# Pinning every engine of a hybrid-decoder step to an order planned from measured durations

## The chip, the cores and the metric

One core of a Trainium2 chip runs one program. Its engines are named as in the profile: PE (matrix products; PEld loads the stationary operand), DVE (vector), ACT (scalar), POOL (GpSimd) and SP (which here only issues DMAs). Each takes its instructions strictly from its own queue, in the order in which the program holds them. The metric is the device time of one execution in microseconds (us), median of several runs.

## The reference

One inference step of one layer, for a prompt of 512 positions and 8 sample positions with the same weights, width 1024, all fp32:

```
proj = rms_norm(x) @ w_in                  # 3 x (q,k,v of 512), r,k,v of 1024, loras, two gates of 1024
o_a  = three dilated-window attentions (8 heads x 64), merged by softmax of their log-sums
# RWKV-7, 16 heads x 64, token by token:
sa = S @ (-kk_t)
S  = S * w_t + outer(sa, kk_t * a_t) + outer(v_t, k_t)
y_t = S @ r_t
o_b = (group_norm(y) + bonus) * gate
x   = x + (sigmoid(gate_a) * (o_a @ w_proj_a) + sigmoid(gate_b) * (o_b @ w_proj_b)) @ w_out
x   = x + (silu(h @ w_gate) * (h @ w_up)) @ w_down         # h = rms_norm(x), width 2816
y   = rms_norm(x)
```

The sample positions also read a key/value cache of 128 rows for each attention group and a matrix state for each RWKV head. New keys, values, shift and states are outputs.

## The kernel before

**Layout and the wide products.** Activations lie with features on the 128 partitions and the 520 positions (512 + 8) along the free axis, in two halves of 260 columns. Each weight matrix is cut into blocks of 128 output features. An fp32 product is made of three faster ones: a block's weights `raw` (512 KB, loaded by SP) are split by ACT into a rounded copy `whi` and by DVE into the rest `wlo = raw - whi`, the activations are held as two such parts (`hh`, `hl`; later `fh`, `fl`, `h2h`, `h2l`), and PE adds up hh·whi, hl·whi and hh·wlo. A block is thus 8 x 3 products for each half, 48 *wide* products of 128x128 weights by 260 columns, into a PSUM tile `mm`. `raw`, `whi` and `wlo` have two buffers each, so the split of a block runs while PE works on the block before. In order the blocks are: 36 of attention, 3 of loras, 24 of RWKV (k, r, v of each pair of heads, called p0 to p7), 16 of gates (g0 to g15), w_proj_a, w_proj_b, w_out, then the FFN.

**The small products.** Between the blocks stand generators with products of other shapes, and of transposes, which also take PE out of its wide shape: attention scores (`ch<-qk`), transposes (`ax<-ident,..`) and the RWKV work of each pair. For a pair, `pair(p)` makes AR, BK and the tiles GH on DVE and PE; `solve(p)` inverts small triangular matrices by 31 steps of two DVE instructions (`xt = X·LT`, `X = X + xt`), each needing the one before, with DMA round trips before (TD, LT) and after (TE, GH) on SP's queue; `chain(p)` walks over 8 chunks: PE VTr·GH and AR·AR, ACT to GH, PE GH·KB, DVE to AR, then the next chunk. `merge()` joins the three attention groups; its tiles `oo` and `fb` are loaded by POOL and used at once by DVE (`oo`, `oac`). `sample_group` works on the cache (`kt`, `sc`, `so`).

**What sets the order.** The main generator `play(jobs)` and the small generators are woven together while the program is written: `Weave.run` keeps an estimated clock for each engine (`Clocks`), and steps the generator whose inputs are ready. Every engine call goes through `Unit.__getattr__.call` (line 380, `r = f(*a, **k)`), which prices it, moves the clocks and emits it; the profile therefore shows nearly every instruction under L380, and tiles are told apart by name. The order in which the calls are made is the priority of an instruction; the framework's scheduler then fixes each engine's queue from priorities and its own costs. The constants TIMED and PIN are 0, so neither of the two other ways of setting an order is in use.

```
def wsplit(w, raw, k0, k1, cols=128):
    hi, lo, raw = (t[:, k0:k1, :cols] for t in (*w, raw))
    S.copy(out=hi, in_=raw)
    V.tensor_tensor(out=lo, in0=raw, in1=hi.bitcast(FP), op=ALU.subtract)
```

Of the kernel before, what the change touches and what calls it, by code (L numbers as in the profile page):

```python
# [1 line left out]

# [37 lines left out]
MERGE_AT = -1  # L40
SAMPLE_AT = -1
PLAIN = 4
EARLY = 3
FETCH = 2
SOLVERS = 2
# [1 line left out]
GRAIN = 2  # L47
SOLVE = 3
AHEAD = 0
TIMED = 0  # L50
PIN = 0
WARM = 0.65
TURNS = 4
L_SEM = 0.2

# [170 lines left out]
class Clocks:  # L226


    def __init__(self):
        self.t = dict(PE=0.0, DVE=0.0, ACT=0.0, POOL=0.0, SP=0.0)  # L230
        self.gaps = {e: [] for e in self.t}
        self.work = []
        self.tick, self.columns, self.hot = 0, 0.0, False
        self.done, self.used, self.prev = {}, {}, {}

    @staticmethod
    def region(x):
# [9 lines left out]

    @staticmethod
    def last(d, engine, r=None):
        t = 0.0  # L250
        for q, (end, by, late) in d.items():
            if r is None or (q[0] < r[1] and r[0] < q[1] and q[2] < r[3] and r[2] < q[3]):
                t = max(t, end + (late if by != engine else 0.0 if by == "PE" else 0.12))
        return t

    def free(self, name, engine, r=None):

        if name not in self.done and name in self.prev:
            name, r = self.prev[name], None
        return max(self.last(d.get(name, {}), engine, r) for d in (self.done, self.used))  # L260

    def at(self, x, engine="PE"):

# [33 lines left out]
            del self.work[0]  # L297
        return sum(w for _, w in self.work) / 3.4

    def run(self, engine, outs, ins, price, issue=None, late=L_SEM):  # L300
        start = max([self.at(x, engine) for x in ins if x.name in self.done] +
                    [self.free(x.name, engine, self.region(x)) for x in outs])
        start = self.place(engine, start, price if issue is None else issue)
        end = start + price
        for x, d in [(x, self.used) for x in ins] + [(x, self.done) for x in outs]:
            d.setdefault(x.name, {})[self.region(x)] = end, engine, late
        return start


class Pool:  # L310


    def __init__(self, pool, ck):
        self.pool, self.ck, self.hist = pool, ck, {}

    def tile(self, shape, dtype, name=None, tag=None, bufs=1):
        t = self.pool.tile(shape, dtype, name=name, tag=tag or name, bufs=bufs)
        h = self.hist.setdefault(tag or name, [])
        if len(h) >= bufs:
            self.ck.prev[t.name] = h[-bufs]  # L320
        h.append(t.name)
        return t

# [6 lines left out]
class Unit:  # L330


    def __init__(self, name, engine, tc, ck, keep=None):
        self.name, self.engine, self.tc, self.ck, self.keep = name, engine, tc, ck, keep

    def price(self, op, outs, ins):
        n = max(x.free_size() for x in outs + ins)
        if self.name == "ACT":
            return 0.06 + n / 1200
        if self.name == "POOL":  # L340
            return 0.25 + n / 480
        if self.name != "PE":
            return 0.07 + n / 960
        n = outs[0].free_size()
        if op == "transpose":
            return 0.054 + n / 2400
        if ins[0].dtype == FR:
            return max(0.054, n / 2400)
        if ins[0].partition_size() > 64:
            return 0.085 + 4 * max(0, n - 32) / 2400  # L350
        return max(0.054, 0.028 + 2 * n / 2400)

    def __getattr__(self, op):
        f = getattr(self.engine, op)

        def call(*a, **k):
            aps = list(a)
            outs = [k[x] for x in ("out", "accum_out") if x in k] or [aps.pop(0)]
            ins = [x for x in aps + [v for n, v in k.items() if n not in ("out", "accum_out")] if isinstance(x, bass.AP)]
            if op == "dma_start":  # L360
                kb = outs[0].nbytes() / 1e3
                pool = self.name == "POOL"
                t = self.ck.run(self.name, outs, ins, (2.7 if pool else 1.6) + kb / 360, 1.04 if pool else 0.45, 0.8)
            else:
                if op == "matmul":
                    ins = ins[::-1] if ins[0] is k.get("rhs") else ins
                p = self.price(op, outs, ins)
                if self.name == "PE":
                    self.ck.beat(self.ck.t["PE"])
                    w = outs[0].free_size() * (4 if ins[0].dtype == FP else 1) / 2400 * ins[0].partition_size() / 128  # L370
                    if op == "transpose":
                        w = 0.0
                    t = self.ck.run(self.name, outs, ins, p if self.ck.hot else 2 * p)
                    self.ck.beat(t, w)
                    self.ck.work.append((t, w))
                else:
                    t = self.ck.run(self.name, outs, ins, p)
            if TIMED:
                self.tc.cur_priority = int(t * TIMED)
            r = f(*a, **k)  # L380
            return self.keep(r) if self.keep else r
        return call


# [81 lines left out]
def program(tc, I, O):  # L466
    nc = tc.nc
    ck = Clocks()
    V, S, G, SY = (Unit(n, e, tc, ck) for n, e in (("DVE", nc.vector), ("ACT", nc.scalar), ("POOL", nc.gpsimd), ("SP", nc.sync)))

    E = Unit("PE", nc.tensor, tc, ck, tc.keep_in_program_order if PIN else None)
    X = mybir.AxisListType.X
    ctx = ExitStack()
    wv = Weave(ck, tc)
# [2 lines left out]
    def nm(s):  # L477
        uid[0] += 1
        return f"{s}_{uid[0]}"

    def pool(name, stack, **kw):
        return Pool(stack.enter_context(tc.tile_pool(name=name, bufs=1, reuse_waits="tile", **kw)), ck)

    cp = pool("const", ctx)
    wp = pool("w", ctx)
    mmp = Pool(ctx.enter_context(tc.tile_pool(name="mm", bufs=1, space=PSUM)), ck)
    axp = Pool(ctx.enter_context(tc.tile_pool(name="ax", bufs=1, space=PSUM)), ck)
    chp = Pool(ctx.enter_context(tc.tile_pool(name="ch", bufs=1, space=PSUM)), ck)
    drp = Pool(ctx.enter_context(tc.tile_pool(name="dr", bufs=1, space=DRAM)), ck)

    def const(name, shape, src=None, eng=None):
        t = cp.tile(shape, FP, name=name)
# [3 lines left out]
    def bank():  # L496
        return axp.tile([128, 512], FP, name=nm("ax"), tag="ax", bufs=3)
# [28 lines left out]
    class Part:  # L526


        def __init__(self, i):
            self.i = i  # L530
# [173 lines left out]
    def norm0():  # L704
        banks = yield from norm_r(n0, [acc0], slice(0, NT), TB, "n0")
        for a, b, pb in banks:
            S.copy(out=rs0[:, a:b], in_=pb[:, :b - a])
        wv.set("rs0")
        for k in range(KD):
            t = n0.tile([128, NT], FP, name=nm("hn"), tag="sq0", bufs=2)  # L710
            V.scalar_tensor_tensor(out=t[:], in0=xt[:, k], scalar=feat[:, F_MIX, k:k + 1], in1=rs0[:],
                                   op0=ALU.mult, op1=ALU.mult)
            split(hh[:, k], hl[:, k], t[:], (V, G)[k % 2])
            yield (hl[:, k],)
# [278 lines left out]
    rw = {}  # L993
# [78 lines left out]
    def gates2():  # L1072
        raw = lora_load(0, 2)
        for p in range(NP):
# [5 lines left out]
            yield lo, st3, BANK  # L1080
# [51 lines left out]
    def pair(p):  # L1132
# [7 lines left out]
        yield lo, BANK  # L1140
# [4 lines left out]
        yield (BANK,)  # L1145
        za = small([(hi[:, 1], LA), (lo[:, 1], LA)])
        ta = full("ta")
        for c in range(2):
# [341 lines left out]
    def merge():  # L1490
# [3 lines left out]
        for i in range(2):  # L1494
            yield stat, BANK
            ps = bank()
            for b in range(4):
                E.transpose(ps[:8, b * 128:(b + 1) * 128], stat[:, 0, i, b], ident[:])
            S.copy(out=nat[:, i], in_=ps[:8].rearrange("p (l r) -> p r l", r=4))
            ps = bank()  # L1500
# [467 lines left out]
```

## Time and profile before

| | |
|---|---|
| median of 3 runs (lowest, highest) | 1315.46 us (1314.71, 1316.59) |
| the profiled execution's own time | 1316.53 us |
| its span, first to last instruction | 1314.8 us |
| busy: PE, DVE, ACT, POOL | 1264.7, 843.7, 610.6, 175.0 us |
| mean granted clock of PE | 0.983 |

The profiled execution is 1.1 us above the median, and 1.7 us of it lie outside the span. I cut the span into four stretches: I, to 359 us (attention blocks, loras, first pairs); II, 359 to 558 us (18 blocks, pairs mostly overlapping each other); III, 558 to 838 us (24 blocks: the last pairs, gates, w_proj_a, w_proj_b up to the point where little but wide products is left); IV, 838 us to the end (rest, almost wholly FFN). The borders are the starts of the splits (`wlo`) of the 46th, 64th and 88th weight block, counted in order on DVE, so that the same points can be found in the changed program.

### The profile page before, as it was taken

What the parts mean: (1) busy time and instruction counts of PE and PEld (TensorE: products, weight loads), DVE (VectorE), ACT (ScalarE), POOL (GpSimd) and SP (SyncE); (2) the same over time, 40 slices, a digit from 0 to 9 for tenths busy, and PEclk for the clock granted to TensorE, in tenths of its full rate; (3) what the DMA queues carried; (4) which work ended last, traced back from release to release, by engine and by line L of the source; (5) the groups of instructions that cost most, each with busy time, mean ns of one, the idle gap of its engine ahead of it and who ended that gap; (6) DMA issues with size and microseconds to landing.
All of it is one profiled execution on the core that took longest, in us unless ns stands there. A gap on an engine that the chain in (4) does not pass through costs nothing.

```text
span 1314.8 us, 29468 instructions
## 1 busy us (share of the span) xinstructions
PE 1264.7 (96%) x11738; PEld 1197.5 (91%) x11738; DVE 843.7 (64%) x2221; ACT 610.6 (46%) x1554; POOL 175.0 (13%) x261
## 2 busy tenths in 40 slices
PE   7999999999989989999999999999999999999996
PEld 7998999989978878888888888999999999999996
DVE  6956866954869998886986665555843444332333
ACT  5244244366656656675785665334433232222220
POOL 1300100100223332121123122110200000000000
PEclk9999999999989999997999999999999999999998
DMA  6523654634245554543245454552222222223331
GB/s 215 158 94 96 213 178 146 221 112 172 69 131 136 152 147 141 143 156 97 77 139 168 123 175 157 182 192 85 81 97 97 97 89 89 97 93 89 89 101 65
DMA packets 92137, 169.48 MB, mean 129 GB/s; under 512 B 42416, under 2 KB 47568, under 8 KB 92000
## 3 DMA queue, kind: packets, MB, share of 16 engines
q1 hardware_dynamic: 60880, 102.46, 24.6%
q0 software_dynamic: 14512, 46.47, 11.5%
q10 hardware_dynamic: 16608, 18.68, 4.3%
q8 instruction: 92, 1.51, 0.5%
q14 instruction: 45, 0.37, 0.1%
HBM read 133.20 MB, written 27.94 MB: 123 GB/s over the span
## 4 chain that ended last, share of the span: by engine, by line
PE 64%; DVE 15%; issue 9%; DMA 6%; ACT 4%; POOL 1%; SPq 1%; ACTq 0%; DVEq 0%; POOLq 0%
PE mm L380 51%; PE ax L380 8%; PE ch L380 5%; DVE wlo L380 2%; DVE X L380 1%; DVE xt L380 1%; DMA fb<-FD 1%; DMA sw<-raw 1%; ACT KB L380 1%; DVE k L380 1%; DMA raw<-w_in 1%; SPq L380 1%; DVE raw L380 1%; DVE qk L380 1%; DVE GH L380 1%
## 5 line engine op out<-in xcount | busy, mean ns | idle before, releaser
L380 PE MATMUL mm<-hh,whi 128*128 128x260 f32 x1136 | 340.2, 299 | 0.8 <-ACT gt L380 0.8
L380 PE MATMUL mm<-hh,wlo 128*128 128x260 f32 x1136 | 325.4, 286 | 4.3 <-DVE wlo L380 4.3
L380 PE MATMUL mm<-hl,whi 128*128 128x260 f32 x1136 | 325.7, 287 | 0.0
L380 ACT CAST whi<-raw 128x1024 fp32r<-128x1024 f32 (+1 forms) x165 | 170.1, 1032 | 324.4 <-PE mm L380 290.6
L380 DVE TENSOR_TENSOR wlo<-raw,whi 128x1024 fp32r<-128x1024 f32 (+1 forms) x165 | 197.9, 1199 | 140.2 <-ACT whi L380 137.0
L380 PEld LDWEIGHTS mm<-hh,whi 128*128 128x128 f32 x1136 | 215.7, 190 | 13.3 <-issue 6.0
L380 PEld LDWEIGHTS mm<-hh,wlo 128*128 128x128 f32 x1136 | 215.4, 190 | 6.5 <-DVE wlo L380 5.8
L380 PEld LDWEIGHTS mm<-hl,whi 128*128 128x128 f32 x1136 | 215.5, 190 | 1.4 <-issue 0.2
L380 PE MATMUL mm<-h2l,whi 128*128 128x260 f32 x608 | 171.5, 282 | 0.0
L380 PE MATMUL mm<-h2h,wlo 128*128 128x260 f32 x608 | 171.4, 282 | 0.0
L380 PE MATMUL mm<-h2h,whi 128*128 128x260 f32 x608 | 171.4, 282 | 0.0
L380 PEld LDWEIGHTS mm<-h2h,wlo 128*128 128x128 f32 x608 | 114.5, 188 | 0.0
L380 PEld LDWEIGHTS mm<-h2l,whi 128*128 128x128 f32 x608 | 114.4, 188 | 0.0
L380 PEld LDWEIGHTS mm<-h2h,whi 128*128 128x128 f32 x608 | 114.4, 188 | 0.0
L380 PE MATMUL mm<-fh,wlo 128*128 128x260 f32 x388 | 109.6, 282 | 0.0
L380 PE MATMUL mm<-fh,whi 128*128 128x260 f32 x388 | 109.5, 282 | 0.0
L380 PE MATMUL mm<-fl,whi 128*128 128x260 f32 x388 | 109.5, 282 | 0.0
L380 PEld LDWEIGHTS mm<-fh,whi 128*128 128x128 f32 x388 | 73.1, 188 | 0.0
L380 PEld LDWEIGHTS mm<-fl,whi 128*128 128x128 f32 x388 | 73.0, 188 | 0.0
L380 PEld LDWEIGHTS mm<-fh,wlo 128*128 128x128 f32 x388 | 72.9, 188 | 0.0
L380 DVE TENSOR_TENSOR xt<-X,LT 128x60 f32<-128x60 f32 (+24 forms) x248 | 60.3, 243 | 3.6
L380 DVE TENSOR_TENSOR X<-X,xt 128x60 f32<-128x60 f32 (+24 forms) x248 | 57.6, 232 | 3.8
(390 smaller groups left out, 2588.8 us busy)
## 6 DMA issues: line engine op xcount, KB each, us to landing
raw<-w_in SPq DMA_DIRECT2D x77, 512.0 KB, 3.7
raw<-w_gate SPq DMA_DIRECT2D x22, 512.0 KB, 3.2
raw<-w_up SPq DMA_DIRECT2D x22, 512.0 KB, 3.2
raw<-w_down SPq DMA_DIRECT2D x16, 512.0 KB, 3.5
kt<-kcache POOLq DMA_DIRECT2D x24, 256.0 KB, 3.7
kt<-vcache POOLq DMA_DIRECT2D x24, 256.0 KB, 3.5
sw<-raw ACTq DMA_DIRECT2D x64, 65.0 KB, 3.6
GD<-gt ACTq DMA_DIRECT2D x16, 260.0 KB, 3.0
```

The source lines that it names most:

```text
L380: r = f(*a, **k)
```

## The change

Each call is now also recorded. `Unit` hands an `Op` (engine, price, issue time, delay until others see the result, PE tile shape) to a `Plan`; `Plan.add` finds from the regions read and written what it must follow. At the end of `program`, `Plan.schedule` simulates all five queues from those prices, and the resulting order is pinned: each instruction gets a dependency without a semaphore on the one before it on its engine. The price formulas are replaced by ones fitted to durations of traces (a DVE instruction 0.155 us + 1 us per 960 columns, and so on). `LAP` says how far two instructions of one engine overlap (DVE 0.083 us), and it is applied both to any two neighbours and to two of which one needs the other. All engines take the earliest-recorded instruction that is ready; only PE chooses differently: `choose` keeps small products in groups. While PE is in the wide shape, it goes on with wide products until a small one has been ready for HOLD = 2.0 us; once out, it takes small ones as long as any is ready; and it does not leave wide products while the share of recent work is under WARMTH = 0.42. The emitted instructions and tiles are the same in kind and number (PE has 10076 matrix products either way). The weave's clocks use the new prices too, and a few generators wait at other places, so pairs of heads start at other blocks.

```diff
+HOLD = 2.0
+WARMTH = 0.42
-TIMED = 0
-PIN = 0
-L_SEM = 0.2
+LAP = {"DVE": 0.083, "ACT": 0.092}
+HOP = {"PE": 0.2, "DVE": 0.04, "ACT": 0.04, "POOL": 0.1, "SP": 0.03}
...
+    def schedule(self):
...
+                if whole:
+                    same = op.engine == o.engine and op.late >= 0.04
+                    t = end - LAP.get(op.engine, 0.0) if same else end if o.engine is None else end + op.late + (0.2 if o.engine == "POOL" else 0.03)
...
+            k = self.choose(ready[e], t, ck) if e == "PE" else heapq.heappop(ready[e])
...
+    def choose(self, ready, t, ck):
+        ops = self.ops
+        small = [k for k in ready if ops[k].shape != (128, 128) or ops[k].turn]
+        wide = len(small) < len(ready)
+        k = min(ready)
+        if small and wide:
+            away = ck.shape != (128, 128) or ck.turned
...
+            if warm < WARMTH and t > 20:
+                k = min(i for i in ready if i not in small)
+            elif away or min(ops[i].ready for i in small) < t - HOLD:
+                k = min(small)
+            else:
+                k = min(i for i in ready if i not in small)
...
         if self.name != "PE":
-            return 0.07 + n / 960
+            return 0.155 + n / 960 + (0.05 if op == "scalar_tensor_tensor" else 0.08 if more else 0)
...
+    for ins in plan.schedule().values():
+        for a, b in zip(ins, ins[1:]):
+            tc.add_manual_dep(b, a.name, mybir.DependencyInfo(mybir.DependencyClass.NoSync, mybir.DependencyReason.DATA),
+                              reason="order")
```

Three places show how the queues change. The first is PE's queue in the stretch of the pairs, before: `ch` rows are steps of a chain (GH and KB, or VTr and GH), `mm` rows the wide products of the block that PE works on.

```order
L380 MATMUL mm_7059<-hh,whi_6972 128x260
L380 MATMUL ch_7101<-VTr_4556,GH_4409 64x64
L380 MATMUL ch_7101<-VTr_4556,GH_4410 64x64
L380 MATMUL ch_7101<-AR_4293 64x64 x2
L380 MATMUL mm_7059<-hl,whi_6972 128x260
L380 MATMUL mm_7059<-hh,wlo_6973 128x260
L380 MATMUL mm_7059<-hh,whi_6972 128x260
L380 MATMUL mm_7059<-hl,whi_6972 128x260
L380 MATMUL mm_7059<-hh,wlo_6973 128x260
L380 MATMUL ch_7101<-GH_4409,KB_4539 64x64
L380 MATMUL ch_7101<-GH_4410,KB_4539 64x64
L380 MATMUL mm_7059<-hh,whi_6972 128x260
```

In the changed kernel PE's queue at such a place:

```order
L603 MATMUL mm_6868<-hh,wlo_6711 128x260
L603 MATMUL mm_6868<-hh,whi_6710 128x260
L603 MATMUL mm_6868<-hl,whi_6710 128x260
L603 MATMUL ch_6803<-GH_4374,KB_4485 64x64
L603 MATMUL ch_6803<-GH_4375,KB_4485 64x64
L603 MATMUL ch_6810<-GH_4887,KB_5009 64x64
L603 MATMUL ch_6810<-GH_4888,KB_5009 64x64
L603 MATMUL mm_6868<-hh,wlo_6711 128x260
L603 MATMUL mm_6868<-hh,whi_6710 128x260
L603 MATMUL mm_6868<-hl,whi_6710 128x260
L603 MATMUL mm_6868<-hh,wlo_6711 128x260
```

Two steps of two different chains (`ch_6803`, `ch_6810`) now stand together between the wide products, where before one chain's steps left the wide shape twice with five wide products between. Over the program PE leaves the wide shape for products of another tile shape 143 times instead of 193 (stretch II: 44 instead of 63, III: 53 instead of 91), and goes from one small shape straight to another 110 times instead of 70.

The second place is DVE's queue at the merge of the attention groups, near the start of stretch II, before: `oac`, `oo` use the loads of POOL, `wlo` is the split of the next weight block, `DN`, `r` belong to a pair.

```order
L380 TENSOR_TENSOR oac_4632<-oo_4373,fb_4375 128x4x128
L380 SCALAR_TENSOR_TENSOR tw_4629<-smask,tw_4629 128x512
L380 TENSOR_TENSOR oo_4640<-oo_4640,fb_4642 128x512
L380 TENSOR_TENSOR oac_4632<-oac_4632,oo_4640 128x4x128
L380 TENSOR_SCALAR DN_4729<-ax_4720 64x4 x2
L380 SCALAR_TENSOR_TENSOR r_4691<-pb_4690,mu,r_4691 128x511
L380 SCALAR_TENSOR_TENSOR r_4691<-shift,mu,r_4691 128x8
L380 TENSOR_SCALAR DN_4729<-ax_4720 64x4 x2
L380 TENSOR_TENSOR wlo_4717<-raw_4572,whi_4716 128x1024
```

And in the changed kernel:

```order
L603 TENSOR_TENSOR oac_4657<-oo_4425,fb_4427 128x4x128
L603 TENSOR_SCALAR sg_4757<-k_4614,feat 128x8
L603 TENSOR_TENSOR wlo_4640<-raw_4463,whi_4639 128x1024
L603 TENSOR_SCALAR sd_4558<-ax_4563 128x8
L603 RECIPROCAL sd_4558<-sd_4558 128x8
L603 SCALAR_TENSOR_TENSOR sg_4246<-pv_4573,sd_4558 128x8
L603 TENSOR_TENSOR sd_4558<-sg_4246,ax_4563 128x16
L603 TENSOR_TENSOR ys<-sd_4558,pv_4573 128x8
L603 TENSOR_TENSOR ys<-sd_4558,ys 128x8
L603 TENSOR_TENSOR sd_5075<-sg_4757 128x8
L603 SCALAR_TENSOR_TENSOR tw_4654<-smask,tw_4654 128x512
L603 TENSOR_TENSOR oo_4659<-oo_4659,fb_4661 128x512
```

The split now stands after one product of the merge instead of after three.

The third place is the solver, DVE's queue in stretch II, before: two instructions `xt`, `X` are one of its 31 steps.

```order
L380 TENSOR_TENSOR xt_4898<-X_4617,LT_4616 128x28
L380 TENSOR_TENSOR oac_4632<-oac_4632,oo_4920 128x4x128
L380 TENSOR_TENSOR X_4617<-X_4617,xt_4898 128x28
L380 TENSOR_TENSOR wlo_4993<-raw_4859,whi_4992 128x1024
L380 TENSOR_TENSOR xt_4901<-X_4617,LT_4616 128x54
L380 SCALAR_TENSOR_TENSOR k_4938<-pb_4937,mu,k_4938 128x511
L380 TENSOR_TENSOR X_4617<-X_4617,xt_4901 128x2x27
L380 SCALAR_TENSOR_TENSOR k_4938<-shift,mu,k_4938 128x8
L380 TENSOR_TENSOR xt_4904<-X_4617,LT_4616 128x52
L380 TENSOR_TENSOR GH_4884<-ax_4960,wmask 128x512
L380 TENSOR_TENSOR X_4617<-X_4617,xt_4904 128x2x26
L380 TENSOR_TENSOR GH_4885<-ax_4967,wmask 128x512
```

And in the changed kernel:

```order
L603 TENSOR_TENSOR xt_4664<-X_4501,LT_4500 128x31
L603 TENSOR_TENSOR X_4501<-X_4501,xt_4664 128x31
L603 TENSOR_TENSOR xt_4667<-X_4501,LT_4500 128x30
L603 TENSOR_TENSOR X_4501<-X_4501,xt_4667 128x30
L603 TENSOR_TENSOR xt_4670<-X_4501,LT_4500 128x29
L603 TENSOR_TENSOR X_4501<-X_4501,xt_4670 128x29
L603 TENSOR_TENSOR xt_4673<-X_4501,LT_4500 128x28
L603 TENSOR_TENSOR X_4501<-X_4501,xt_4673 128x28
L603 TENSOR_TENSOR xt_4676<-X_4501,LT_4500 128x54
L603 TENSOR_TENSOR X_4501<-X_4501,xt_4676 128x2x27
L603 TENSOR_TENSOR xt_4679<-X_4501,LT_4500 128x52
L603 TENSOR_TENSOR X_4501<-X_4501,xt_4679 128x2x26
```

Where other work stood between the steps, they now follow one another without a break. Over the program, DVE instructions that need the one directly before them in its queue go from 409 to 871; in stretch II from 90 to 339. There the queue also becomes longer, 709 instructions instead of 540: the pairs start some blocks earlier (one solver more, 31 x 2 instructions, and one pair's front more), and the last group of the sample cache stands there (8 `kt`, 8 `so`). Stretch III has 529 instead of 702, and the gate blocks g11 to g15 (before: g14, g15) come after the fourth block of w_proj_a. PE has 168 more small products in II (729 instead of 561) and 179 fewer in III (788 instead of 967), and 12 wide products moved from III to II.

More of the change, by code (lines that the diff above doesn't have):

```diff
@@ L1 @@
+import heapq
 from contextlib import ExitStack
@@ L234, in __init__ @@
         self.done, self.used, self.prev = {}, {}, {}
+        self.order, self.begun = {}, {}
+        self.floor = {}
+        self.shape, self.turned = (128, 128), False
     @staticmethod
@@ L249, in last @@
     def last(d, engine, r=None):
-        t = 0.0
+        t, wake = 0.0, 0.2 if engine == "POOL" else 0.03
         for q, (end, by, late) in d.items():
             if r is None or (q[0] < r[1] and r[0] < q[1] and q[2] < r[3] and r[2] < q[3]):
-                t = max(t, end + (late if by != engine else 0.0 if by == "PE" else 0.12))
+                t = max(t, end + (late + wake if by != engine or late < 0.04 else -LAP.get(by, 0.0)))
         return t
     def free(self, name, engine, r=None):
-        if name not in self.done and name in self.prev:
-            name, r = self.prev[name], None
-        return max(self.last(d.get(name, {}), engine, r) for d in (self.done, self.used))
+        n = self.prev.get(name)
+        return max([self.floor.get(name, 0.0), self.begun.get(self.order.get(name), 0.0)] +
+                   [self.last(d.get(name, {}), engine, r) for d in (self.done, self.used)] +
+                   [self.last(d.get(n, {}), engine) for d in (self.done, self.used)])
     def at(self, x, engine="PE"):
@@ L298, in warmth, with through, shift @@
         return sum(w for _, w in self.work) / 3.4
-    def run(self, engine, outs, ins, price, issue=None, late=L_SEM):
+    def through(self, names):
+        return max([max(self.last(d.get(n, {}), "SP") for d in (self.done, self.used)) for n in names] + [0.0])
+    def shift(self, shape, op):
+        wide, t = shape == (128, 128), 0.0
+        if shape != self.shape:
+            t = 0.19 if wide else 0.09
+        elif wide and self.turned and op != "transpose":
+            t = 0.09
+        self.shape, self.turned = shape, op == "transpose"
+        return t
@@ L301, in run @@
+    def run(self, engine, outs, ins, price, issue=None, late=None):
+        late = HOP[engine] if late is None else late
         start = max([self.at(x, engine) for x in ins if x.name in self.done] +
                     [self.free(x.name, engine, self.region(x)) for x in outs])
+        for x in ins:
+            if x.space == PSUM:
+                start = max(start, self.last(self.used.get(x.name, {}), engine))
         start = self.place(engine, start, price if issue is None else issue)
         end = start + price
+        for x in outs:
+            self.begun.setdefault(x.name, start)
@@ L305, in run, with __init__ @@
         for x, d in [(x, self.used) for x in ins] + [(x, self.done) for x in outs]:
-            d.setdefault(x.name, {})[self.region(x)] = end, engine, late
-        return start
+            d, key = d.setdefault(x.name, {}), (*self.region(x), engine)
+            d[key] = max(d.get(key, (0.0,))[0], end), engine, late
+        return start
+class Op:
+    def __init__(self, engine, ins, price, issue, late, shape, turn, work):
+        self.engine, self.ins, self.price, self.issue, self.late = engine, ins, price, issue, late
+        self.shape, self.turn, self.work = shape, turn, work
+        self.after, self.left, self.ready = [], 0, 0.0
@@ L310, with __init__ @@
 class Pool:
-    def __init__(self, pool, ck):
-        self.pool, self.ck, self.hist = pool, ck, {}
+    def __init__(self, pool, ck, plan, before=(0.0, None)):
+        self.pool, self.ck, self.plan, self.hist, self.before = pool, ck, plan, {}, before
     def tile(self, shape, dtype, name=None, tag=None, bufs=1):
@@ L319, in tile @@
         if len(h) >= bufs:
-            self.ck.prev[t.name] = h[-bufs]
+            self.ck.prev[t.name] = self.plan.prev[t.name] = h[-bufs]
+        self.ck.floor[t.name] = self.before[0]
+        if self.before[1] is not None:
+            self.plan.floor[t.name] = self.before[1]
+        if h:
+            self.ck.order[t.name] = self.plan.order[t.name] = h[-1]
         h.append(t.name)
@@ L359, in call @@
             ins = [x for x in aps + [v for n, v in k.items() if n not in ("out", "accum_out")] if isinstance(x, bass.AP)]
+            shape, work = None, 0.0
             if op == "dma_start":
@@ L362, in call @@
                 pool = self.name == "POOL"
-                t = self.ck.run(self.name, outs, ins, (2.7 if pool else 1.6) + kb / 360, 1.04 if pool else 0.45, 0.8)
+                p, issue, late = (3.4 if pool else 2.7) + kb / 300, 0.56 if pool else 0.36, 0.03
+                self.ck.run(self.name, outs, ins, p, issue, late)
             else:
@@ L468, in program @@
     ck = Clocks()
-    V, S, G, SY = (Unit(n, e, tc, ck) for n, e in (("DVE", nc.vector), ("ACT", nc.scalar), ("POOL", nc.gpsimd), ("SP", nc.sync)))
-    E = Unit("PE", nc.tensor, tc, ck, tc.keep_in_program_order if PIN else None)
+    plan = Plan(ck)
+    V, S, G, SY = (Unit(n, e, tc, ck, plan) for n, e in (("DVE", nc.vector), ("ACT", nc.scalar), ("POOL", nc.gpsimd), ("SP", nc.sync)))
+    E = Unit("PE", nc.tensor, tc, ck, plan)
     X = mybir.AxisListType.X
@@ L1499, in merge @@
             S.copy(out=nat[:, i], in_=ps[:8].rearrange("p (l r) -> p r l", r=4))
+            yield stat, BANK
             ps = bank()
```

215 lines of the change are left out of this document (184 added, 31 removed).

## The prediction

> **What bounds the kernel now.** I read the head of the page first (busy time of each engine, the 40 slices, the shares of the chain of waits), then cut the span into the four stretches.
>
> ```profile
> PE 1264.7 (96%) x11738; PEld 1197.5 (91%) x11738; DVE 843.7 (64%) x2221; ACT 610.6 (46%) x1554; POOL 175.0 (13%) x261
> PEclk9999999999989999997999999999999999999998
> PE 64%; DVE 15%; issue 9%; DMA 6%; ACT 4%; POOL 1%; SPq 1%; ACTq 0%; DVEq 0%; POOLq 0%
> ...
> 0.00:359.00 359.00, 346.10 (x2843) 328.01 (x2844) 254.45 (x639) 174.33 (x461) 43.58 (x70) 1.00 0.47 153
> 359.00:558.00 199.00, 184.11 (x1901) 165.91 (x1900) 173.50 (x540) 121.77 (x328) 56.43 (x80) 0.97 0.50 140
> 558.00:838.00 280.00, 268.84 (x3101) 238.94 (x3100) 203.28 (x704) 181.37 (x579) 58.08 (x88) 0.96 0.44 135
> 838.00:1314.80 476.80, 465.67 (x3900) 464.67 (x3898) 212.45 (x341) 133.12 (x188) 16.94 (x23) 0.99 0.31 102
> ```
>
> The window rows give length, then busy time of PE, PEld, DVE, ACT, POOL, the granted clock and DMA. PE bounds the kernel as a whole, but not evenly. In IV it is busy for 465.67 of 476.80 us with wide products alone, and the change has nothing to take there. In II DVE is busy for 173.50 of 199 us, almost as long as PE: there either can set the end. In III DVE has 77 us to spare.
>
> What can be won on PE are waits, a halved clock and changes of tile shape. The waits of PE and of DVE, by what ended them:
>
> ```profile
> PE mm L380 <- ACT whi L380: 7.6, 3, 7.1
> PE mm L380 <- DVE wlo L380: 5.1, 6, 1.4
> PE ch L380 <- ACT GH L380: 4.0, 4, 2.4
> ...
> DVE AR L380 <- PE ch L380: 14.7, 24, 1.8
> DVE oac L380 <- DMA fb<-FD: 6.1, 3, 5.4
> ...
> 592.82 0.33 PE L380 MATMUL ch<-VTr,GH 64*64 64x64 f32 x4 [1.45 <-DVE AR L380]
> ...
> 385.70:392.50 6.80, 6.42 (x30) 5.71 (x29) 5.43 (x15) 0.77 (x1) 2.00 (x3) 0.50 0.40 136
> 593.90:610.90 17.00, 17.00 (x101) 14.95 (x100) 10.81 (x30) 6.49 (x15) 4.70 (x6) 0.50 0.28 84
> 699.70:703.10 3.40, 3.40 (x15) 3.20 (x14) 3.37 (x8) 0.39 (x1) 3.33 (x4) 0.50 0.12 19
> ```
>
> No single wait is large. But a wait of 1.45 us at 592.82 is followed by 17.00 us in which the clock was 0.50: half of them, 8.5 us, are lost, more than the wait. In III 20.4 us ran at half clock, a loss of 10.2.
>
> **A change of tile shape.** The timeline of PE, start and length of each group:
>
> ```profile
> 500.64 0.28 PE L380 MATMUL mm<-hh,wlo 128*128 128x260 f32 x1
> 500.85 0.34 PE L380 MATMUL ch<-GH,KB 128*64 128x64 f32 x4
> 501.11 0.39 PE L380 MATMUL mm<-hh,whi 128*128 128x260 f32 x1
> 501.34 0.28 PE L380 MATMUL mm<-hl,whi 128*128 128x260 f32 x1
> 501.46 0.28 PE L380 MATMUL mm<-hh,wlo 128*128 128x260 f32 x1
> ...
> 592.98 0.28 PE L380 MATMUL ch<-AR 64*64 64x64 f32 x4
> ```
>
> Wide products start 0.12 us apart. From 500.64 to 501.46 pass 0.82 us with three wide products (0.36), so four small ones between them cost 0.46. Four that follow others of their shape take 0.16 (592.82 to 592.98, above). A round trip out of the wide shape is therefore 0.46 - 0.16 = 0.30 us. A change from one small shape to another no row shows alone: it lies between 0 and 0.30, and I take half, 0.15.
>
> **The grouping on PE.** Round trips fall by 19 in II and 38 in III: -5.7 and -11.4 us. Changes between small shapes rise by 40 and 3: +6.0 and +0.5. In I seven more round trips cost 2.1. So grouping alone is worth some 9 us, all of it on PE's path only where PE is the bound.
>
> **Work moved between stretches.** What one small product costs I take from III: of 268.84 us busy, 1172 wide products take 140.6 (x 0.12), 91 round trips 27.3, 47 small changes 7.0, half clock 10.2; the other 83.7 us are 967 small products, 0.087 us each. PE's work in II becomes 184.11 + 168 x 0.087 + 12 x 0.12 - 5.7 + 6.0 = 200.4 us. III without its waits and its clock loss touched: 280 - 179 x 0.087 - 1.4 - 11.4 + 0.5 = 252.1 us.
>
> **DVE in stretch II: the price of the new order there.** The groups of DVE that grow, and neighbours in the timeline, independent ones first, then a solver's steps:
>
> ```profile
> L380 DVE TENSOR_TENSOR xt<-X,LT 128x60 f32<-128x60 f32 (+24 forms) x248 | 60.3, 243 | 3.6
> L380 DVE TENSOR_TENSOR X<-X,xt 128x60 f32<-128x60 f32 (+24 forms) x248 | 57.6, 232 | 3.8
> L380 DVE TENSOR_TENSOR GH<-ax,wmask 128x512 f32<-128x512 f32 x32 | 21.8, 684 | 6.8 <-PE ax L380 6.6
> L380 DVE TENSOR_TENSOR kt<-kt,sc 128x512 f32<-128x512 f32 x24 | 16.8, 703 | 5.1 <-DMA kt<-vcache 5.1
> ...
> 379.27 0.69 DVE L380 SCALAR_TENSOR_TENSOR ta<-ta,k 128x520 f32<-128x520 f32 x1
> 379.88 0.68 DVE L380 TENSOR_TENSOR AR<-r,E 128x512 f32<-128x512 f32 x1
> 380.49 0.74 DVE L380 SCALAR_TENSOR_TENSOR BK<-ta,feat,tw 128x512 f32<-128x512 f32 x1
> ...
> 479.05 0.23 DVE L380 TENSOR_TENSOR xt<-X,LT 128x63 f32<-128x63 f32 x1
> 479.31 0.22 DVE L380 TENSOR_TENSOR X<-X,xt 128x63 f32<-128x63 f32 x1
> 479.57 0.22 DVE L380 TENSOR_TENSOR xt<-X,LT 128x60 f32<-128x60 f32 x1
> ```
>
> Independent neighbours overlap: 379.27 + 0.69 is 379.96, and the next has started at 379.88, 0.08 earlier. A needed one waits for the end and a little more: 479.05 + 0.23 is 479.28, and the next starts at 479.31, 0.03 later. So a dependent neighbour costs 0.11 us more than an independent one. The plan's LAP gives both -0.083: it holds the rows of the solver, one behind the other, to be as cheap as any, and interleaves nothing.
>
> In II the added rows are one solver (31 xt, 31 X: 14.7 us by the means above), 8 kt and 8 so (11.1, at about 0.69), 5 GH (3.4) and the rest of a pair's front, 91 rows of mostly 128x512 or 128x8, 22.2 us by the means of their own groups: 51.4 us in all. Of the 169 added rows and those reordered, 249 more are dependent neighbours (+0.034 each, 8.5 us), and 80 fewer overlap (6.6 us). DVE's busy time in II: 173.50 + 51.4 + 8.5 + 6.6 = 240.0 us. That is 39.6 more than PE's 200.4: **DVE becomes the bound of II**, and PE waits there for `wlo`. What of the 25.5 us in which DVE now idles in II (199 - 173.50; rows above: AR behind PE, oac behind the loads) remains is open: nothing up to all of it. I take 2.4, the longest single wait of the chain row (ch <- ACT GH), since with 40 us less PE work than DVE work something is nearly always ready: II = 242.4, ends 233 (240 less 7 us, should half of the overlap terms be wrong) and 265.5.
>
> [...]
>
> **Stretch III.** DVE falls to 203.28 - 53.4 (the rows that left, by the same means) + 110 more dependent neighbours x 0.034 + 285 fewer overlaps x 0.083 = 177.3 us, far under PE's. PE is the bound, and of its 280 - 268.84 = 11.2 us of waits and 10.2 of lost clock I let all return but one wait of 1.45 us: the plan starts pairs earlier, so a chain's step is ready before its group. 252.1 - 20.0 = 232.1; ends 226 (small changes free, all won) and 248 (waits and clock stay but for 4 us).
>
> **Stretch I.** DVE has 24 rows of the first norm and of rope ahead of a split where 12 stood, so PE waits some 3 us more early on, and +2.1 of shape changes; against these stand waits on `whi` and `wlo` (the two rows above, 12.7 us in the whole program, 5 of them here). I cost it at nothing: 359. **Stretch IV** keeps its products and order: 476.8.
>
> **What covers the rest.** SP's queue is in order, and a load of `raw` now stands behind TD, LT, TE and GH of two pairs.
>
> ```profile
> raw<-w_in SPq DMA_DIRECT2D x77, 512.0 KB, 3.7
> ```
>
> A load lands in 3.7 us, and a block of PE takes 199 / 18 = 11 in II: two buffers cover it; without that cover a late load costs up to 7. POOL's queue (oo, fb for the merge) has 56.43 us of work in II; the split that stood behind three merge instructions now stands behind one, so the 5.4 us of the longest oac wait hits one split fewer. ACT is at 121.77 of 199 in II and stays off the path.
>
> **Sum.** 359 + 242.4 + 232.1 + 476.8 = 1310.3 us of span, against 1314.8; with the 1.7 outside it 1312.0; the profiled execution stood 1.1 above the median, so 1311 us. The kernel's runs lie within 2 us of each other, and I count 0.2%, 2.6 us, as no measurable change.
>
> **Rivals.** *The plan holds* (0.22): dependent rows cost no more, or PE-side slack swallows it: 249 x 0.117 = 29 us less in II, 1282 us. For it: only II is DVE-bound, and splits stand early in the queue. Against: the 102 neighbours xt, X in the trace are all 34 to 35 ns apart, end to start.
>
> *The pinned queue stalls* (0.24): a fixed queue can't step round a late DMA, so II keeps DVE's 25.5 us of idle time on top of 240: 265.5, and 1311 + 23.1 = 1334. It decides from 7 us of idle time on, where II and III are together over the 479 us of before. PE then idles (265.5 - 200.4) / 18 = 3.6 us per block, more than the 1.45 us that went ahead of the half clock. Against it: 200.4 us of PE work fit into 265 down to a mean clock of 0.76, against 0.97 in the row of II, so the stall must be DVE's own. [...]
>
> *The last chain ends III* (0.08): each of p7's 16 groups may be held for HOLD, 16 x 2.0 = 32 us, and g11 to g15, 5 blocks x 48 x 0.12 = 29 us, cover all but 3: 1314, no measurable change. Against: a group already out of the wide shape takes it at once.
>
> **How the numbers follow.** My own sum has 0.46. By its ends it lies between 1300 and 1322: 0.27 of it below 1312.8, 0.13 within the bound, 0.06 above 1318.1. Faster: 0.22 + 0.27 = 0.49. Same: 0.13 + 0.08 = 0.21. Slower: 0.24 + 0.06 = 0.30. The range goes from 1280 to 1335, to the middles of the outer rivals, which leaves about half of each, 0.2, outside.
>
> **What will show it.** Right: between the 46th and the 64th split over 235 us, with DVE busy over 0.95 and PE's waits on wlo there near 40 us; between the 64th and the 88th under 240 at a clock of 0.99; xt to X still 0.03 after the end. Wrong: II near 210 with DVE at 0.9 (the dependent rows are hidden), or DVE waits on DMA and ACT in II over 10 us, or half-clock windows in II that slow PE below DVE.

## The result: 8% slower, lost in the first two stretches

The changed kernel takes 1420.7 us (median of 4 runs, 1418.44 to 1424.13) against 1315.09 for the kernel before; the ratio is 1.0811, 95% interval 1.0778 to 1.0844. The profiled execution has a span of 1422.3 us. Its page, the lines that answer to those shown of before:

```profile
PE 1293.8 (91%) x11738; PEld 1226.0 (86%) x11738; DVE 875.0 (62%) x2221; ACT 612.5 (43%) x1554; POOL 169.7 (12%) x261
PEclk9989999999988888998998899999999999999998
```

The four stretches, cut at the same splits of weight blocks (the 46th, 64th and 88th), columns as in the prediction:

```profile
0.00:400.70 400.70, 364.14 (x2909) 340.63 (x2910) 262.96 (x645) 179.23 (x476) 43.30 (x73) 0.96 0.44 138
400.70:674.80 274.10, 219.26 (x2182) 198.74 (x2182) 233.28 (x711) 143.49 (x404) 65.15 (x92) 0.86 0.41 112
674.80:946.50 271.70, 246.22 (x2765) 223.12 (x2766) 167.01 (x531) 157.00 (x489) 45.76 (x74) 0.94 0.41 128
946.50:1422.30 475.80, 464.19 (x3889) 463.48 (x3887) 211.70 (x340) 132.81 (x188) 15.46 (x22) 0.99 0.31 102
```

I is 41.7 us longer than before (359), II 75.1 (199), III 8.3 shorter (280), IV 1.0 shorter (476.8). III has less work than before, so its 271.7 us are no gain against the forecast, as shown below. In II neither engine is full: PE is busy for 219 of 274 us at a clock of 0.86, DVE for 233. Between 10 and 1290 us, 20 stretches at half clock add up to 146.8 us; before there were 5, 34.1 us. What PE waits for (us in total, times, longest):

```profile
PE ch L603 <- DVE AR L603: 18.4, 10, 5.5
PE ax L603 <- DVE sg L603: 15.0, 2, 9.8
PE mm L603 <- DVE wlo L603: 12.0, 7, 7.8
PE ax L603 <- DVE AR L603: 8.0, 4, 4.4
```

And where DVE waits for DMAs, with the first of these waits before the change in the last row:

```profile
DVE raw L603 <- DMA sw<-raw: 22.7, 7, 6.6
DVE T L603 <- DMA GH<-TE: 8.8, 4, 4.0
DVE X L603 <- DMA TE<-X: 7.6, 3, 3.9
...
DVE raw L380 <- DMA sw<-raw: 4.9, 6, 2.5
```

The largest waits are put down not to weights but to small tiles of the pairs; all 12.0 us for `wlo` lie in stretch I. One of them on PE's timeline:

```profile
415.19 0.28 PE L603 MATMUL mm<-hl,whi 128*128 128x260 f32 x1
425.24 1.19 PE L603 MATMUL ax<-AR,BK 64*128 64x128 f32 x4 [9.77 <-DVE sg L603]
426.36 0.58 PE L603 MATMUL mm<-hh,whi 128*128 128x260 f32 x1
```

DVE's timeline in that time, solver steps of a pair, then the AR that PE waits for, and behind it the split of the block that PE is in:

```profile
415.89 0.23 DVE L603 TENSOR_TENSOR xt<-X,LT 128x63 f32<-128x63 f32 x1
416.15 0.22 DVE L603 TENSOR_TENSOR X<-X,xt 128x63 f32<-128x63 f32 x1
416.41 0.22 DVE L603 TENSOR_TENSOR xt<-X,LT 128x60 f32<-128x60 f32 x1
...
424.41 0.68 DVE L603 TENSOR_TENSOR AR<-r,E 128x512 f32<-128x512 f32 x1
...
426.16 1.22 DVE L603 TENSOR_TENSOR wlo<-raw,whi 128x1024 fp32r<-128x1024 f32 x1
```

The same time as a window, and the stretch at half clock that overlaps it:

```profile
415.20:425.30 10.10, 0.33 (x4) 0.15 (x2) 9.51 (x32) 2.57 (x6) 1.23 (x2) 0.65 0.10 27
418.20:431.90 13.70, 6.66 (x26) 5.55 (x27) 12.72 (x31) 3.12 (x7) 2.35 (x4) 0.50 0.31 97
```

PE waits for 9.77 us, though wide products of the same block stand right behind in its queue and start without a wait of their own at 426.36: the order has put AR·BK ahead of them. (The row names `sg`, DVE's next row after AR; the product reads AR, which is done at 425.09.) DVE is busy nearly all that time (9.51 of 10.10 us) with rows that stand ahead of the AR instruction. Only a part of the block was ready, though. Its `whi` was done at 411.17, but its `wlo` is split at 426.16, behind AR, so the 16 of its 48 products that read `wlo` could not have run either. Two had run before the wait; the other 30 are worth 3.6 us at 0.12 each, an estimate. So DVE's late queue would soon have held PE here by its split as well, unless other work stood ready. The clock falls to half during the wait, at 418.20, 2.7 us after PE's last product has ended, and stays there for 13.70 us; in the last 6.7 of them PE has work again and does it at half clock: between 430.1 and 431.8 wide products start 0.22 us apart, against 0.12 before the wait.

Another kind stands in I: DVE waits 6.56 us for a DMA, its timeline shows nothing between the two rows. The load that it waits for was issued on SP's queue at 83.0 us and took 5.8 to land.

```profile
81.12 1.22 DVE L603 TENSOR_TENSOR wlo<-raw,whi 128x1024 fp32r<-128x1024 f32 x1
88.89 0.70 DVE L603 TENSOR_TENSOR raw<-raw,rope 128x520 f32<-128x520 f32 x1 [6.56 <-DMA sw<-raw]
```

### The profile page after: what moved, and what is told of

The parts are those of the page before. It is cut to its first block, busy times and chain, and to the rows that moved or that the text cites. A ratio compares the mean times of both kernels' runs of the same rounds, so it can differ in the third digit from the quotient of the medians.

```text
span 1422.3 us, 29482 instructions
## 1 busy us (share of the span) xinstructions
PE 1293.8 (91%) x11738; PEld 1226.0 (86%) x11738; DVE 875.0 (62%) x2221; ACT 612.5 (43%) x1554; POOL 169.7 (12%) x261
## 5 line engine op out<-in xcount | busy, mean ns | idle before, releaser
L603 PE MATMUL mm<-hh,whi 128*128 128x260 f32 (+1 forms) x1136 | 338.1, 298 | 7.7 <-ACT v L603 4.9
L603 PE MATMUL mm<-hh,wlo 128*128 128x260 f32 (+1 forms) x1136 | 336.4, 297 | 4.3 <-DVE wlo L603 4.2
L603 PE MATMUL mm<-hl,whi 128*128 128x260 f32 (+1 forms) x1136 | 336.9, 297 | 0.0
L603 DVE TENSOR_TENSOR wlo<-raw,whi 128x1024 fp32r<-128x1024 f32 (+1 forms) x165 | 200.9, 1218 | 183.6 <-ACT whi L603 180.2
L603 PEld LDWEIGHTS mm<-hh,whi 128*128 128x128 f32 (+1 forms) x1136 | 225.0, 198 | 11.7 <-ACT v L603 5.1
L603 PEld LDWEIGHTS mm<-hh,wlo 128*128 128x128 f32 (+1 forms) x1136 | 224.0, 197 | 11.8 <-DVE wlo L603 5.7
L603 PEld LDWEIGHTS mm<-hl,whi 128*128 128x128 f32 (+1 forms) x1136 | 224.8, 198 | 4.2 <-issue 2.2
L603 DVE TENSOR_TENSOR xt<-X,LT 128x60 f32<-128x60 f32 (+24 forms) x248 | 55.6, 224 | 9.0 <-DMA LT<-TD 2.1
```

## The experiments

Four theories. A: the plan prices a DVE instruction that needs its neighbour as if it overlapped with it, so it stacks them, and DVE falls behind the order planned for the others. B: the groups of small products are bad in themselves. C: the plan prices DMAs too short. D: the weave, with its new prices and yields, emits the work in a worse order, whatever is pinned. In each run below the ratio is to the kernel before on the same chip, with its 95% interval; the medians of before were 1309 to 1313 us.

**First set: one part at a time.** The plan's price of dependent DVE instructions (e1); no groups (e2); no pinning (e3); only PE pinned (e4).

```diff
 e1 -  t = end - LAP.get(op.engine, 0.0) if same else ...
    +  t = end + 0.034 if same and op.engine == "DVE" else end - LAP.get(op.engine, 0.0) if same else ...
 e2 -  k = self.choose(ready[e], t, ck) if e == "PE" else heapq.heappop(ready[e])
    +  k = heapq.heappop(ready[e])
 e3 -  for ins in plan.schedule().values():
    +  for ins in ():
 e4 +  for ins in [plan.schedule()["PE"]]:
```

> The plan alone is changed: where a DVE instruction needs the one before it on DVE, the plan lets it start 0.034 us after that one's end, as measured in the traces, instead of 0.083 us before it. Dependent neighbours on DVE fall from 710 (strictly counted) to 411, in stretch II from 339 to 104, and everything else is planned and pinned as in the changed kernel; PE leaves its wide shape 151 times instead of 143. Theory A (the plan's wrong price of dependent DVE instructions puts DVE on the path, and PE then waits and loses its clock): most of the 105 us come back, 1290 to 1340, stretch II under 215 us, fewer than 10 half-clock windows. Theory B (groups of small products keep PE's activity low and hold the chains' steps): 1395 to 1425. Theory C (any order pinned from such optimistic estimates stalls on late DMAs): 1380 to 1425. Theory D (the weave emits the work in a worse order, whatever is pinned): 1395 to 1425.

> PE takes the earliest recorded ready product, like the other engines, so small products are not kept in groups; all else as in the changed kernel (PE leaves its wide shape 162 times instead of 143, dependent DVE neighbours 732 instead of 710). Theory A: about as slow as the changed kernel, 1405 to 1435. Theory B: 1315 to 1360. Theory C and D: 1400 to 1430.

> The plan is not applied: the program is emitted as in the changed kernel, and the framework's scheduler sets every queue, as before (190 round trips, 348 dependent DVE neighbours, 67 of them in stretch II; the pairs still start as early as in the changed kernel, with 681 DVE instructions in II). Theories A, B and C: near the kernel before, 1300 to 1335. Theory D: 1390 to 1425.

> Only PE's queue is pinned to the plan's order, with its groups; the other queues are left to the framework's scheduler (143 round trips, 393 dependent DVE neighbours, 95 in II). Theory A: 1300 to 1345, since DVE is spread out again. Theory B: 1390 to 1425, since the groups are the same. Theory C: in between, 1340 to 1390, as PE alone is rigid. Theory D: 1390 to 1425.

| run | median us | ratio to before |
|---|---|---|
| e1, dependent DVE price | 1365.1 | 1.0389 (1.0342 to 1.0436) |
| e2, no groups | 1410.14 | 1.0758 (1.0712 to 1.0804) |
| e3, no pinning | 1349.72 | 1.029 (1.0246 to 1.0334) |
| e4, PE alone pinned | 1395.41 | 1.0639 (1.0606 to 1.0672) |

No theory has it alone. One constant in the plan gives 55.6 of the 105.6 us back, less than theory A expected. Without groups 10 come back (7 by the ratios). With nothing pinned, 38 of the loss are still there: the emission. Pinning as planned costs the other 71. e3 lies between its two ranges, e4 where B and D expected it, but e2 speaks against B as the main cause, and e3 against D: PE's order costs 46 us over e3 even where DVE's is free. The first correction in the four stretches' windows, of e1:

```profile
0.00:383.70 383.70, 353.50 (x2904) 331.40 (x2905) 257.90 (x643) 179.56 (x476) 47.26 (x73) 0.98 0.46 145
383.70:626.60 242.90, 216.70 (x2211) 195.77 (x2210) 213.82 (x699) 145.30 (x408) 66.13 (x92) 0.90 0.45 125
```

II falls from 274.10 to 242.90 with nearly the same rows on DVE (699 for 711): its busy time falls by 19.5 us and its idle time by 11.7. II stays far over the 215 that A expected.

**Second set: the other price, and the emission.** e5 adds slower DMAs to e1's plan. e6 pins nothing and corrects the same dependent price in the weave's clocks. e7 lets the weave emit as before and pins the unaltered plan, e8 pins the plan with both corrections on it.

```diff
 e5, e8 +  p, issue = p + 2.0, 0.6          # each dma_start, in the plan only
 e6     -  ... if by != engine or late < 0.04 else -LAP.get(by, 0.0)
        +  ... if by != engine or late < 0.04 else 0.034 if by == "DVE" else -LAP.get(by, 0.0)
 e7, e8 -  ck = Clocks()
        +  ck = OldClocks()                 # clocks, prices and yields of before
```

> The first experiment's plan (dependent DVE instructions priced as measured) with slower DMAs in the plan alone: 2.0 us more from issue to landing (2.7 became 4.7 us plus size; the traces have medians of 2 to 4.2 and a slowest tenth of 4 to 6.5 us) and 0.6 instead of 0.36 us for an issue. The weave emits as in the changed kernel. Theory C (the order stalls where a DMA lands later than planned): 1315 to 1345. Theory D (the rest of the loss is the weave's emission, of which the unpinned run showed 38 us): 1345 to 1365. Theory A alone (dependents were all of the plan's fault): as the first experiment, 1358 to 1370.

> No queue is pinned, as in the third experiment; the weave's clocks alone are changed: a DVE instruction that needs one of DVE starts 0.034 us after its end instead of 0.083 us before it. The pairs then start later again: stretch II has 565 DVE instructions (before 540, changed kernel 709, unpinned 681). Theory A extended to the weave (it took the solver for cheap, so pairs started too early and DVE got more work in II than fits): back to 1305 to 1325. If the 38 us of the unpinned run come from other parts of the emission (yields, other prices): 1340 to 1355.

> The weave emits as in the kernel before (its prices, clocks and yields; without pinning, all five queues come out word for word as before), and the plan of the changed kernel, unaltered, pins all queues: 143 round trips, 668 dependent DVE neighbours. Pinning by itself, then. Theory A and C (the plan's prices are at fault whatever is emitted): 1360 to 1400, some 70 us over before, as between the unpinned run and the changed kernel. Theory D (the emission is the fault): 1300 to 1330.

> As the run beside it, with both corrections of the plan (dependent DVE neighbours +0.034 us, DMAs 2.0 us later and 0.6 us per issue): 140 round trips, 431 dependent DVE neighbours. Theory A and C: the plan is no longer optimistic and the grouping's gain shows, 1290 to 1315. If pinning in groups is bad in itself (theory B, or rigid order whatever the prices): 1325 to 1365.

| run | median us | ratio to before |
|---|---|---|
| e5, both prices | 1342.29 | 1.0214 (1.0159 to 1.0268) |
| e6, no pinning, weave's dependent price | 1332.42 | 1.0142 (1.0086 to 1.0198) |
| e7, emission of before, plan unaltered | 1408.21 | 1.0708 (1.064 to 1.0776) |
| e8, emission of before, both prices | 1330.1 | 1.012 (1.0066 to 1.0173) |

e5 lies where C expected it and e6 between its two ranges. e7 is slower than any theory had it. e8 misses the range of A and C and lies in that of the other case, that groups or a rigid order cost something at any prices.

e7 against e8 settles the main question: with the emission of before, pinning costs 95 us with the plan's own prices and 17 with both corrections. D is not what makes the pinned kernel slow. Of the two, the DMA line is rather a margin than a correction: it plans 4.9 us for a 65 KB load, while the `sw<-raw` loads of the changed kernel landed after 2.6 us (ACT's queue) and 2.0 (SP's) in the median. Whether its 2.0 us of landing or its longer issue does the work was not separated. The emission costs 38 us where nothing is pinned (e3) and 12 once the plan is corrected (e5 against e8). Of the 38, e6 gives 17 back: the weave, too, took the solver for cheap and started pairs too early (stretch II has 565 DVE instructions in e6, 681 in e3, 540 before).

**Third set: what is left of the pinned loss.** All on e8. e9 takes the groups out (the whole of `choose`, so HOLD and WARMTH together), e10 prices each DVE instruction 0.05 us longer (0.205 for 0.155), e11 pins PE alone.

> The weave's emission of before and the corrected plan (as the eighth run, 1330), but PE takes the earliest recorded ready product: no groups, 185 round trips instead of 140. Groups good (the steps price each round trip at 0.30 us, so 45 of them 13 us, less 40 small changes): slower than the eighth run, 1335 to 1345. Theory B (groups hold the chains' steps and lower the activity of PE): faster, 1312 to 1325.

> As the eighth run, with a margin on DVE: each DVE instruction priced 0.05 us longer in the plan (0.205 instead of 0.155 us plus size), about what DVE's instructions took over their price along the chain of that run (29.7 us in 624 instructions). Dependent DVE neighbours fall from 431 to 324. Theory A and C (what remains of the loss is optimism on DVE): 1310 to 1325. If the rest has another cause: 1326 to 1340.

> As the eighth run, but only PE's queue is pinned, DVE, ACT, POOL and SP are left to the framework's scheduler. If rigid queues on the other engines are what still costs: 1305 to 1322. If PE's planned order carries the loss (as in the fourth run, where pinning PE alone cost 46 of 71 us): 1325 to 1345.

e9 took 1319.87 us, ratio 1.0068 (1.0046 to 1.0091): faster, as B expected, where my own pricing of round trips had it slower. e10 took 1324.58, ratio 1.0102 (1.0068 to 1.0136), at the upper end of what A and C expected, and not told apart from e8. e11 took 1358.12, ratio 1.0372 (1.0335 to 1.0409), over both expectations: with the corrected plan, one queue pinned to an order that the others don't follow is worse than all five pinned. With the unaltered plan it was the other way round (e4 1395.41, all five 1420.7).

**Fourth set: the groups, the yields, and whether the prices add up.** e12 is e9 with e10's margin. e13 pins nothing, and takes over only the changed yields. e14 is the changed kernel with e5's DMA line alone. e15 repeats e8 and e16 repeats e9, in one set.

> The weave's emission of before, all queues pinned to the corrected plan, no groups (as the ninth run, 1320) and the margin of 0.05 us on each DVE instruction (as the tenth): 202 round trips, 321 dependent DVE neighbours, 555 DVE instructions in stretch II. If the plan's remaining optimism on DVE is what is left of the loss: 1300 to 1313, a gain over before. If a pinned order gains nothing once its prices are right: 1313 to 1322.

> No pinning, the weave's prices and clocks of before, and only the few changed yields of the changed kernel. The unpinned run with all of the new emission took 1350, and correcting the weave's price of dependent DVE instructions gave 17 of its 38 us back. If the yields carry the other 20: 1328 to 1340. If the other new prices of the weave do: 1308 to 1320.

> The changed kernel with the DMAs alone planned slower (2.0 us more to landing, 0.6 us per issue); dependent DVE instructions stay at the wrong price (721 dependent neighbours, 336 in stretch II). If the two corrections act apart from each other: 1421 - 23 = 1395 to 1402. Theory A as the root (queues are late because of DVE, so later DMAs help little): 1405 to 1425. Theory C as the root: 1350 to 1385.

> The eighth run again (before's emission, corrected plan, groups), beside its twin without groups on the same chip, since the two were measured in different sets. Groups cost: 8 to 12 us over the twin. No difference: within 3 us.

> The ninth run again (before's emission, corrected plan, no groups), the twin of the run beside it. Groups cost: 1316 to 1322, and 8 to 12 us under the twin.

| run | median us | ratio to before |
|---|---|---|
| e12, corrected, margin, no groups | 1317.3 | 1.0056 (1.0037 to 1.0076) |
| e13, yields alone, no pinning | 1321.35 | 1.0095 (1.0055 to 1.0134) |
| e14, DMA price alone | 1394.36 | 1.0619 (1.0588 to 1.065) |
| e15, corrected, groups | 1331.58 | 1.0148 (1.0117 to 1.0179) |
| e16, corrected, no groups | 1319.05 | 1.0063 (1.0044 to 1.0082) |

The effects of the two prices add up: the DMA price alone gives 26 us (1420.7 to 1394.36, just under the range expected for this case), on top of the other 23 (1365.1 to 1342.29). Groups cost 12.5 us, e15 over e16, with intervals apart. The yields alone cost 12 us, between the two ranges, of the 20 that e6 left of the emission; the remaining few are not told apart. Where the time of the groups goes is seen in stretches II and III together. The window of e15, with groups:

```profile
360.70:853.20 492.50, 450.20 (x4965) 407.45 (x4963) 386.00 (x1244) 305.27 (x901) 119.67 (x169) 0.94 0.45 134
```

And of e16, without:

```profile
357.20:839.80 482.60, 456.64 (x4993) 407.68 (x4991) 382.31 (x1239) 305.42 (x905) 111.81 (x168) 0.96 0.46 136
```

With groups PE is busy for 6.4 us less there, at a lower clock even so (2.7 us less over the whole program, as some of its work lies in I). So the round trips save something. But PE idles for 42.3 us instead of 26.0. That held small products make others wait, and these PE, would explain it; no run shows it step by step.

The parts account for most of the loss: 55.6 us (e1) and 22.8 more (e5) for the two prices, 12.2 for the emission (e5 against e8), 12.5 for the groups, 103.1 of 105.6 in all, though put together from several sets. What remains without groups is 0.6% (e16). One price that no run altered may be in it: the plan still lets an ACT instruction overlap by 0.092 us with one that it needs. No version beat the kernel before: e12, the best that the experiments pointed to, is 0.6% slower, as expected if a pinned order gains nothing.

## Why the prediction was wrong, point by point

Forecast was 1311, in a range to 1335; measured 1420.7. The sum had a span of 1310.3 us, and it was 1422.3. Of the 112.0 us between them 41.7 lie in I, 31.7 in II and 39.6 in III; IV took 1.0 less.

- **The price of dependent neighbours: right.** 0.03 us after the end it was taken to be, and the changed kernel shows it unaltered (416.15 + 0.22 is 416.37, and the next starts at 416.41, in the rows above). It was named as the plan's error, and it is the largest single one: 55.6 us. So the first rival, which rested on rows costing no more, falls. In the same queue `sg`, which does not need AR, starts at 425.01, 0.08 us before AR's end (424.41 + 0.68). So here too a row that waits for its neighbour costs 0.11 us more than one that does not.
- **DVE's load in II: right.** 240.0 predicted, 233.28 measured, with 711 rows where 709 were counted. Of the 240.0, the 8.5 us after dependent neighbours are gaps, which the page does not count as busy, so 231.5 is what compares.
- **"I take 2.4" for DVE's idle time on top of it: this step failed.** It was 274.10 - 233.28 = 40.8 us. The waits that the profile lists in it are 26.0 us, against 20.7 before; the rest is short gaps. So the waits did not vanish, they grew: 16.4 us were for DMAs, 5.2 for ACT, 4.4 for PE. The argument was that with more DVE work than PE work something is nearly always ready on DVE. In a pinned queue the next row has to be ready, not some row; the longest of these waits, of `X` for the DMA that copies it to TE, took 3.9 us. The upper end of 25.5 us, DVE's idle time before, was no bound either: II took 34.1 us over the 240.0. The sign "DVE waits on DMA and ACT in II over 10 us" came true with 21.6, but with 14.2 it had held before the change too and could tell nothing.
- **PE's waits: right in size, wrong in kind.** I expected some 40 us in II for `wlo`. PE idled for 54.8 us (274.10 - 219.26), by the profile mostly for AR, sg and GH, and not once for `wlo`. In the longest of these waits the split was late too, but hidden by the AR ahead of it. So what held PE there was DVE's queue, as forecast, and it cost more because DVE itself was waiting, mostly for DMAs.
- **"All but one wait return" in III, 20.0 us: failed.** III took 271.70 against 232.1. PE's busy time was 246.22, close to the 240.9 that the steps give with half clock kept (252.1 less 11.2 of waits), and it idled for 25.5 us, more than twice the 11.2 of before, at a clock of 0.94 instead of 0.96. The reason given, that a chain's step is ready before its group, did not hold: in III PE's products `ch` and `ax` waited 13.8 us for AR and sg (5.5 in the longest), and DVE's AR in turn 15.2 us for PE's `ch`.
- **"I cost it at nothing" for I: failed, 41.7 us.** I held the plan's DMA price against no trace there. Before, `sw<-raw` from ACT's queue took 3.6 us to landing in the median and 5.65 at most; the plan's formula gives 2.9. DVE waited 22.7 us for it (4.9 before), 21.9 in e1 and 2.7 in e5, so a plan with more room for DMAs does away with these waits. Late landings are only a part of them: three of the seven ended with loads that took 3.9 to 5.8 us, the other four with loads that landed after 2.0, issued some 0.6 us apart where the plan has 0.36. Of the 41.7 us in I, e1 gives 17.0 back (383.70) and e5 another 19.4 (364.3).
- **The weave: missed as a term.** I counted that pairs start earlier, as work moved between stretches, but not that the new emission costs by itself: 38 us unpinned (17 of them come back with the weave's dependent price, and the yields alone cost 12) and 12 in the pinned kernel.
- **The grouping: the sign was wrong.** Some 9 us gained in the sum; it costs 7 to 12.5 (e2, e15 against e16). PE's busy time does fall, the idle time that comes with it was left out.
- **The rival "the pinned queue stalls" was the mechanism,** with its condition fulfilled. In II its 265.5 us were not far from 274.10, but I let it act in that stretch alone, on one engine and without the clock, so its 1334 lies 87 us short.
- **The ends were added up wrongly.** The ends given for II and III make 1295 to 1350, not "between 1300 and 1322". The wider ends would not have reached 1420.7 either.
- **The clock: my test came out as wrong.** I let half-clock time fall; it rose from 34.1 to 146.8 us, in 20 stretches instead of 5. The one shown begins in a wait of 9.77 us and lasts 13.70.

## What to carry to other kernels

A pinned order is only as good as its most optimistic price: with a static queue a late row stops all behind it (one AR held PE for 9.77 us, with wide products that were ready behind it), so prices of links between engines and of DMAs should be taken from the slow side of the trace, and neighbours that need each other priced apart from those that don't (e7 to e8: 78 us from two corrections). When judging such a change, price the mismatch, not the plan: for each engine, compare the plan's link prices with the trace, and do not let one engine's load cover the idle time of another. Saving engine time by holding work back did not pay here: PE's busy time fell and its idle time rose by more (e15 against e16).

## What the runs showed of the hardware that I had not expected

In one place PE's clock fell behind waits of 1.13 us at most (the longest ended at 803.36), where PE was fed with small products; in another place like it the clock stayed up. In the changed kernel, the window of 3.4 us before a fall to half, and the stretch after it:

```profile
803.90:807.30 3.40, 2.04 (x64) 1.77 (x64) 1.07 (x1) 3.26 (x10) 1.68 (x3) 1.00 0.76 205
807.30:821.00 13.70, 13.50 (x112) 10.62 (x113) 9.39 (x41) 8.34 (x21) 2.90 (x5) 0.50 0.42 142
```

What PE ran in the first of these, by groups:

```profile
L603 PE MATMUL ax<-VTr,GH 64*64 64x64 f32 x32 | 1.4, 224 | 0.8 <-ACT KB L603 0.8
L603 PE MATMUL ax<-T,GH 32*32 32x32 f32 x32 | 0.7, 192 | 0.0
```

Another window of small products alone in the same kernel, the one after it, and what PE ran in the first:

```profile
745.90:749.30 3.40, 2.11 (x60) 1.91 (x60) 3.40 (x5) 2.93 (x8) 0.00 (x0) 1.00 0.01 2
749.30:752.70 3.40, 3.04 (x24) 2.89 (x25) 2.17 (x9) 3.07 (x19) 0.58 (x1) 1.00 0.91 253
...
L603 PE MATMUL ch<-GH 128*64 128x64 f32 x32 | 1.2, 225 | 0.7 <-DVE AR L603 0.7
L603 PE MATMUL ch<-AR 64*64 64x64 f32 x28 | 1.0, 222 | 0.0
```

And a pair of windows in e15:

```profile
419.80:423.20 3.40, 2.87 (x33) 2.71 (x34) 3.37 (x9) 2.56 (x7) 1.19 (x1) 1.00 0.17 40
423.20:426.60 3.40, 3.40 (x17) 3.18 (x16) 3.37 (x6) 0.33 (x2) 2.70 (x3) 0.50 0.79 245
```

In the first window of the changed kernel PE ran 64 small products and no wide one, was busy for 2.04 us and waited 0.8; the next ran at 0.50. In the second it ran 60 small ones and no wide one, was busy for 2.11 us and waited 0.7; the next kept 1.00. In e15 PE was busy for 2.87 of 3.40 us, with 31 of its 33 products small, and the next window ran at 0.50. So in these three windows neither PE's busy time nor the number of small products tells whether the clock fell. The two windows of the changed kernel differ in tile shape (64x64 and 32x32 against 128x64 and 64x64) and in the longest wait shortly before (1.13 us up to 803.36, 0.75 up to 745.93); which of them decides, if either, was not shown. With groups the stretches at half clock between 10 and 1290 us add up to 61.4 us, without to 41.0 (e15, e16; mean granted clock 0.973 and 0.981). How much of the groups' 12.5 us is clock and how much waiting was not separated.
